# Layer B's second pair of plain projections, five tiles for the reload of the mixer output, and ScalarE's order

## The chip, the cores and the metric

The kernel runs on one NeuronCore of one Trainium2 chip. The metric is the device time of one execution in microseconds (us). TensorE (PE) multiplies matrices, VectorE (DVE), ScalarE (ACT) and GpSimd (POOL) do the elementwise work, SyncE (SP) issues most of the DMAs and ACT's queue some of them. Each engine works through its own list of instructions in order.

## The reference

A decoder trunk of two layers is computed for a prompt of 1024 tokens and 8 sample tokens, 1032 columns in all, at a model width of 1024 and an inner width of 2048, in float32:

```python
hn = rmsnorm(h, norm_mix[i])
# layer A: y = hgrn2_mixer(hn, ...)   chunkwise gated linear recurrence, 8 heads
# layer B: y = chunk_mlp_mixer(hn, ...)
u, v, z = jnp.split(hn @ w_in, 3, axis=-1)
u = gelu(u); v = layernorm(gelu(v), ln_g, ln_b)
s = einsum('gts,bnsgd->bntgd', tril(w_sp), v in chunks of 128) + b_sp
y = (u * s * silu(z)) @ w_out
h = h + y
gate = sigmoid(rmsnorm(h, norm_ple[i]) @ w_ple_gate[i])
h = h + gate * (p[i] @ w_ple_proj[i])
# after both layers: rmsnorm(h, norm_final)
```

Beside the rows of y, the final recurrent states and the last chunk's v rows are returned.

## The kernel before

Activations lie with features on the 128 partitions. The 1032 columns are split into three chunks c = 0, 1, 2 of 384, 384 and 264 columns. Every float32 operand x of a large product is split in two parts, hi (a rounding cast on ScalarE) and lo = x - hi (a subtraction on VectorE or GpSimd), and `mm3` makes three matmuls of it: hi hi, hi lo, lo hi. A weight is treated in the same way by `split_weights`. A projection (`proj`) of one output tile of 128 features and one chunk is thus 8 x 3 = 24 matmuls into one of three PSUM banks that share the tag "mm".

PE's list of instructions is as traced (its schedule is manual). The other engines' lists are put in order by a planner, which simulates the program and takes instructions by priority and expected readiness; `high_priority` moves some forward. Side work that must run between PE's products is written as generators. `Ticks` steps them: `tk.tick()` counts once per half projection or per group, and a generator that yields n goes on n ticks later. The constants SQD, SDEL, NDEL and FDEL are such delays: in `first_norm` SQD is the tick at which a chunk's squares are traced, and SDEL's two numbers are the ticks to the sum over partitions (`norm_sum`, tile pss) and from there to the broadcast (`norm_bc`, tile pbc), after which the normalised rows are split into hi and lo. NDEL does the same for later norms.

The stages that matter here, in order of time:

- The start. p's first projection (`pple`, 12 groups of 6 matmuls, each group emptied from its bank by a ScalarE copy at L301 and stored to DRAM) fills PE while x arrives and is normalised by `first_norm`. Then come the projections fk and qq of head 0, per chunk.
- Layer A, 8 heads. At its end `last_fill` runs p's second projection and the first half of the output projection; `load_zt` brings the mixer output of layer A back from DRAM (tiles ozd), tile by tile, with a cast on ScalarE and a subtraction on VectorE for each.
- Layer B begins while the last norm of layer A is still at work (`norm_rows`, chunk by chunk; chunk 2 last). First one plain pair of v's projections is computed (weights b, MI and MI+1, three chunks each). A Gelu (`vgroup`, L945) makes gv; two ticks later `vstore` transposes it on PE (pt_g, L954), copies it, takes its statistics and stores it. Then `mix` forms sums and differences of the chunks' rows for a Strassen-like scheme and splits them into xm (L900 to L910): four operations and three splits for each of four j, half of them on GpSimd. From then on `unit` computes two output tiles at once, over chunks 0 and 1 by seven products of 12 matmuls in place of eight, and chunk 2 by plain projections. Each unit needs sums of its weights (`load_unit`: four adds on GpSimd, four casts, four subtractions). Units run for the rest of v (m from 2), and then for u and z of each of eight groups g.
- In the last group (g = 7) hooks between the unit's products (`then`) load what the output projection will need: p for layer 1 goes into hh[2], and rows of ozd go into the places of activations that the unit no longer reads. These loads are staged in `wide()` tiles, six buffers named "u", which also hold the gated outputs us until L1147 multiplies them.
- `out_phase` ("ob"): p's last projection (12 groups), with loads of ozd between the groups in stages of three tiles, then the output projection in halves of 8 blocks (tiles ps_o), with the rows of h loaded from DRAM. Then the gate (`ple`) and the final norm.

## Time and profile before

| | us |
|---|---|
| median of 3 runs | 1977.56 (1973.95 to 1980.73) |
| the profiled execution | 1973.68 |
| its span, first to last instruction | 1971.9 |
| PE busy | 1893.8 (96%) |
| VectorE busy | 1182.6 (60%) |
| ScalarE busy | 782.9 (40%) |
| GpSimd busy | 456.8 (23%) |

A row of a timeline gives the start, the length, the engine with line and operation, and, in brackets, how long the engine was idle before it and what released it. Lengths of matmuls are modelled and overlap; how far apart their starts are shows the rate. The granted clock is 1.00 at 2.4 GHz; the lower level is 1.2 GHz. L197 and L196 are the subtraction and the cast inside `split`, L142 and L143 those of `split_weights`, L201 to L203 the three matmuls of `mm3`, and L306 the DMA in `load_split`: many tiles share these lines, so the names of the tiles tell them apart.

### The profile page before, as it was taken

The page shows a single profiled execution, that of the slowest core. Times are in us where ns is not written, and L with a number is a line of the kernel's source. Part 1 is how long each engine was busy: PE and PEld are TensorE (multiplying, and loading weights), DVE is VectorE, ACT ScalarE, POOL GpSimd, SP SyncE. Part 2 cuts the span into 40 slices and gives each one's busy share as a digit, 9 for nine tenths or more (in the row PEclk, how much of TensorE's full clock was granted, in tenths as well). Part 3 has the DMA queues.
Part 4 walks back from the last instruction along what each step waited for, and adds up shares of the span by engine and source line. Part 5 has one row for each costly group of instructions (what it writes and reads, how often), then busy time and mean ns, then how long its engine had stood idle before and what let it go on. Part 6 is the DMA issues. An engine that isn't in the chain of part 4 may idle for free.

```text
span 1971.9 us, 33475 instructions
## 1 busy us (share of the span) xinstructions
PE 1893.8 (96%) x13160; PEld 1852.3 (94%) x13160; DVE 1182.6 (60%) x2610; ACT 782.9 (40%) x1610; POOL 456.8 (23%) x467
## 2 busy tenths in 40 slices
PE   7999999999999998999998899999999996999997
PEld 6999999999999998999998899999999996999997
DVE  5967676776767676311645755587777675311554
ACT  6452535444453536311434544433443344211341
POOL 5110000001000100011323622354444440011221
PEclk8999999999999999999999899999999998999998
DMA  6232322222131326511243333332233238411123
GB/s 207 84 105 71 101 91 79 76 89 97 57 108 59 106 93 217 185 44 44 98 157 111 108 98 92 102 98 95 97 99 105 95 113 262 138 49 44 65 87 107
DMA packets 124076, 203.73 MB, mean 103 GB/s; under 512 B 11600, under 2 KB 96784, under 8 KB 122896
## 3 DMA queue, kind: packets, MB, share of 16 engines
q1 hardware_dynamic: 115280, 191.04, 29.9%
q10 hardware_dynamic: 8640, 10.57, 1.5%
q8 instruction: 103, 1.69, 0.4%
q14 instruction: 53, 0.43, 0.1%
HBM read 148.75 MB, written 52.82 MB: 102 GB/s over the span
## 4 chain that ended last, share of the span: by engine, by line
PE 45%; DVE 7%; DMA 4%; issue 2%; POOL 2%; ACT 2%; SPq 0%; DVEq 0%; POOLq 0%; ACTq 0%
PE ps_proj L202 7%; PE ps_proj L201 7%; PE ps_proj L203 7%; PE ps_o L201 6%; PE ps_o L202 6%; PE ps_o L203 6%; PE ps_d L201 1%; PE ps_d L203 1%; PE ps_d L202 1%; DMA zstg<-ozd 1%; DVE wlo L143 1%; DMA vn<-vraw 1%; DVE bl L197 1%; PE psp L1139 1%; DMA ppd<-pple_t 1%
## 5 line engine op out<-in xcount | busy, mean ns | idle before, releaser
L201 PE MATMUL ps_proj<-bh,whi 128*128 128x384 f32 (+1 forms) x2136 | 689.2, 323 | 8.1 <-ACT pple_t L301 6.7
L202 PE MATMUL ps_proj<-bl,whi 128*128 128x384 f32 (+1 forms) x2136 | 673.3, 315 | 3.8 <-DVE bl L197 2.5
L203 PE MATMUL ps_proj<-bh,wlo 128*128 128x384 f32 (+1 forms) x2136 | 672.9, 315 | 3.1 <-DVE wlo L143 3.1
L201 PEld LDWEIGHTS ps_proj<-bh,whi 128*128 128x128 f32 x2136 | 404.3, 189 | 12.2 <-ACT pple_t L301 6.9
L202 PEld LDWEIGHTS ps_proj<-bl,whi 128*128 128x128 f32 x2136 | 404.8, 190 | 6.6 <-DVE bl L197 3.4
L203 PEld LDWEIGHTS ps_proj<-bh,wlo 128*128 128x128 f32 x2136 | 403.6, 189 | 3.7 <-DVE wlo L143 3.7
L143 DVE TENSOR_TENSOR wlo<-wstg,whi 128x1024 fp32r<-128x1024 f32 x148 | 190.7, 1289 | 152.1 <-ACT whi L142 148.8
L142 ACT CAST whi<-wstg 128x1024 fp32r<-128x1024 f32 x148 | 155.3, 1050 | 130.0 <-PE ps_proj L202 72.3
L234 POOL TENSOR_TENSOR ssq<-ssq,tmp 128x384 f32<-128x384 f32 (+1 forms) x72 | 76.3, 1059 | 419.9 <-ACT tmp L233 372.2
L808 DVE TENSOR_TENSOR h<-h,ps_o 128x384 f32<-128x384 f32 (+1 forms) x48 | 24.5, 511 | 192.9 <-PE ps_o L203 192.9
L142 ACT CAST shi<-ssum 128x512 fp32r<-128x512 f32 x92 | 56.5, 621 | 176.9 <-POOL ssum L172 102.7
L201 PE MATMUL ps_o<-bh,whi 128*128 128x384 f32 (+1 forms) x384 | 123.2, 321 | 2.1 <-ACT pple_t L301 1.6
L202 PE MATMUL ps_o<-bl,whi 128*128 128x384 f32 (+1 forms) x384 | 122.6, 319 | 0.6 <-DVE bl L197 0.6
L233 ACT ACTIVATE tmp<-h 128x384 f32<-128x384 f32 (+1 forms) x72 | 35.3, 490 | 219.5 <-DVE h L808 168.9
L203 PE MATMUL ps_o<-bh,wlo 128*128 128x384 f32 (+1 forms) x384 | 122.4, 319 | 0.0
L143 DVE TENSOR_TENSOR slo<-ssum,shi 128x512 fp32r<-128x512 f32 x92 | 76.7, 833 | 42.9 <-ACT shi L142 42.9
L201 PE MATMUL ps_o<-zh,whi 128*128 128x384 f32 (+1 forms) x288 | 90.0, 313 | 0.0
L202 PE MATMUL ps_o<-zl,whi 128*128 128x384 f32 (+1 forms) x288 | 89.7, 312 | 0.0
L203 PE MATMUL ps_o<-zh,wlo 128*128 128x384 f32 (+1 forms) x288 | 89.7, 311 | 0.0
L589 DVE TENSOR_TENSOR q<-q,t 128x192 f32<-128x192 f32 (+1 forms) x144 | 49.9, 347 | 45.2 <-PE pC L583 43.5
L201 PEld LDWEIGHTS ps_o<-bh,whi 128*128 128x128 f32 x384 | 72.7, 189 | 2.8 <-ACT pple_t L301 2.1
L202 PEld LDWEIGHTS ps_o<-bl,whi 128*128 128x128 f32 x384 | 72.6, 189 | 1.0 <-DVE bl L197 1.0
(278 smaller groups left out, 3904.1 us busy)
## 6 DMA issues: line engine op xcount, KB each, us to landing
wstg<-in_wina SPq DMA_DIRECT2D x48, 512.0 KB, 3.6
wstg<-in_winb SPq DMA_DIRECT2D x48, 512.0 KB, 4.0
zstg<-ozd SPq DMA_DIRECT2D x22, 384.0 KB, 5.7
pj<-ppd SPq DMA_DIRECT2D x16, 516.0 KB, 3.8
S<-in_st SPq DMA_DIRECT2D x16, 512.0 KB, 5.1
vb<-vd SPq DMA_DIRECT2D x16, 512.0 KB, 4.6
out_so_s<-S SPq DMA_DIRECT2D x16, 512.0 KB, 3.4
wstg<-in_wouta SPq DMA_DIRECT2D x16, 512.0 KB, 4.2
```

What stands on the lines that cost most here:

```text
L142: A.copy(hi, src)
L143: V.tensor_tensor(lo, src, hi.bitcast(F32), ALU.subtract)
L197: eng.tensor_tensor(lo, src, hi.bitcast(F32), ALU.subtract)
L201: PE.matmul(ps, wh, xh, start=first, stop=False, skip_group_check=more)
L202: PE.matmul(ps, wh, xl, start=False, stop=False, skip_group_check=more)
L203: PE.matmul(ps, wl, xh, start=False, stop=last, skip_group_check=more)
L233: A.activation(sq[:, :w], src, AF.Square)
L234: eng.tensor_tensor(ssq, ssq, sq[:, :w], ALU.add)
L589: V.tensor_tensor(ql[:, :, 1, :], ql[:, :, 1, :], t2[:, :, 0:1].broadcast_to([P, n, lv]), ALU.mult)
L808: V.tensor_tensor(hr[c][m], hr[c][m], ps[:, :W[c]], ALU.add)
L1139: PE.matmul(pss[:, i, :], vn[:, n0 + i, mm * P:(mm + 1) * P], wst[:, g, :], start=True, stop=True)
```

## The change

- Layer B computes two plain pairs (MI to MI+3) before the first unit, and units of v begin at m = 4. The transposes of these pairs come 4 ticks after the Gelu.
- `mix` becomes a generator that starts once the first pair is done and `norm_rows` has ended. Its operations and the subtractions of its splits all go to VectorE, behind the last norm's last subtraction, one j per tick. The four splits into hh[1] go to VectorE too.
- `load_zt` can issue DMAs `lag` tiles ahead of the cast and can tie each cast behind whatever ScalarE was given last (`keep_in_program_order`: an order of issue, without a wait). The tie is the default and thus holds at the end of layer A also.
- In the last group the rows of ozd are staged in five tiles "zq" of their own, five ahead, without the tie. cv is formed in place in gb.
- `out_phase` allocates its staging pool first, loads one tile after each group with a lag of two, and takes chunk 2's rows 0 to 7 into new tiles and 8 to 15 into hh[2].
- At the start the staging of p has three tiles, pple_t six, the squares of chunks 1 and 2 are tied behind a PSUM copy and behind a split, and SQD, SDEL and NDEL have other delays.

```diff
 NWARM = 12
+ZQ = 5
 FDEL = ((2, 2), (2, 4), (1, 3))
-SQD = (0, 5, 9)
+SQD = (0, 6, 12)
 OD = (4, 4)
-SDEL = ((6, 3), (6, 2), (6, 2))
-NDEL = (((1, 3), (1, 4), (2, 3)), ((2, 4), (2, 6), (2, 6)))
+SDEL = ((6, 4), (7, 2), (5, 2))
+NDEL = (((1, 3), (1, 4), (2, 3)), ((2, 4), (2, 6), (3, 6)))
 OFF = (0, 384, 768)
 W = (384, 384, 264)
 NT = (3, 3, 2)
...
     order += [("g", 0, m) for m in range(KT)]
     order += [("p", 1, 0)]
-    order += [("b", MI), ("b", MI + 1)] + [("B", MI + m) for m in range(2, MI, 2)]
+    order += [("b", MI + m) for m in range(4)] + [("B", MI + m) for m in range(4, MI, 2)]
...
@@ -192,9 +193,11 @@
         return loaded[n]
 
 
+    last = {}
+
     def split(hi, lo, src, eng=V):
-        A.copy(hi, src)
-        eng.tensor_tensor(lo, src, hi.bitcast(F32), ALU.subtract)
+        last["split"] = A.copy(hi, src)
+        last["lo"] = eng.tensor_tensor(lo, src, hi.bitcast(F32), ALU.subtract)
...
 
-    def load_p(ap, l, c, ph, pl):
-        stg = ap.tile([P, 2, 384], F32, name="pstg", bufs=2)
+    def load_p(ap, l, c, ph, pl, bufs=2):
+        stg = ap.tile([P, 2, 384], F32, name="pstg", bufs=bufs)
         nc.sync.dma_start(stg[:, :, :W[c]], pT[l][:, :, OFF[c]:OFF[c] + W[c]])
         ph[c] = ap.tile([P, 2, W[c]], F32R, name=f"ph{c}")
...
                     mm3(ps[:, :W[c]], blk(wh, b), blk(wl, b), ph[c][:, k, :], pl[c][:, k, :], k == 0, k == 1)
                 t = tp.tile([P, 384], F32, name="pple_t", tag=stg[0], bufs=stg[1])
-                A.copy(t[:, :W[c]], ps[:, :W[c]])
+                last["pple"] = A.copy(t[:, :W[c]], ps[:, :W[c]])
                 nc.scalar.dma_start(ppd[l][4 * half + mm][:, OFF[c]:OFF[c] + W[c]], t[:, :W[c]])
...
@@ -306,13 +309,24 @@
         nc.sync.dma_start(stg, src)
         split(hi, lo, stg)
 
-    def load_zt(zt, parts, stage, n=2):
-
-        for c, k0 in parts:
-            zh, zl, nk = zt[c, k0]
-            for k in range(0, nk, n):
-                load_split(zh[:, k:k + n, :], zl[:, k:k + n, :], ozd[c][:, k0 + k:k0 + k + n, :], stage(W[c]))
-                yield
+    def load_zt(zt, parts, stage, n=2, lag=0, tie=True):
+
+
+        todo = [(c, k0, k) for c, k0 in parts for k in range(0, zt[c, k0][2], n)]
+        stg = []
+        for i in range(len(todo) + lag):
+            if i < len(todo):
+                c, k0, k = todo[i]
+                stg.append(stage(W[c]))
+                nc.sync.dma_start(stg[i], ozd[c][:, k0 + k:k0 + k + n, :])
+            if i >= lag:
+                c, k0, k = todo[i - lag]
+                zh, zl, _ = zt[c, k0]
+                hi = A.copy(zh[:, k:k + n, :], stg[i - lag])
+                if tie:
+                    tc.keep_in_program_order(hi)
+                V.tensor_tensor(zl[:, k:k + n, :], stg[i - lag], zh[:, k:k + n, :].bitcast(F32), ALU.subtract)
+            yield
 
...
@@ -366,24 +380,27 @@
 
     load(0)
     ph, pl = [None] * 3, [None] * 3
-    load_p(sp, 0, 0, ph, pl)
-    load_p(sp, 0, 1, ph, pl)
+    load_p(sp, 0, 0, ph, pl, 3)
...
-    fill = pple(0, sp, ph, pl, 0, ("pple_t", 4))
+    fill = pple(0, sp, ph, pl, 0, ("pple_t", 6))
 
     def first_norm(c):
-        yield SQD[c]
+        if c:
+            yield SQD[c]
         sq = sp.tile([P, KT, 384], F32, name="sq0", bufs=2)[:, :, :W[c]]
         for j in range(0, KT, 2):
-            A.activation(sq[:, j:j + 2, :], xs[c][:, j:j + 2, :], AF.Square)
+
+            with tc.issue_after(last["pple" if c == 1 else "split"].ins) if c else ExitStack():
+                A.activation(sq[:, j:j + 2, :], xs[c][:, j:j + 2, :], AF.Square)
             (V if c == 0 else G).tensor_tensor(sq[:, j, :], sq[:, j, :], sq[:, j + 1, :], ALU.add)
             if j:
                 (V if c == 0 else G).tensor_tensor(sq[:, 0, :], sq[:, 0, :], sq[:, j, :], ALU.add)
...
         with ExitStack() as s:
+            st = stage2(pool(s, "zstg"), 3)
             zp = pool(s, "oz")
 
             def load_h(m):
@@ -782,17 +800,13 @@
                     for c in CH:
                         nc.sync.dma_start(hr[c][m], src[:, OFF[c]:OFF[c] + W[c]])
 
-            st = stage2(pool(s, "zstg"), 3)
             for c, k0, nk in parts:
                 zt[c, k0] = (zp.tile([P, nk, W[c]], F32R, name=f"zh{c}_{k0}"),
                              zp.tile([P, nk, W[c]], F32R, name=f"zl{c}_{k0}"), nk)
-            todo = load_zt(zt, late, st)
-            if fill is not None:
-                for i, _ in enumerate(fill):
-                    if i % 2:
-                        tk.tick()
-                        next(todo, None)
-                run(load_zt(zt, [(2, 0)], st))
+            todo = load_zt(zt, late, st, 2, 2 if fill else 0)
+            for _ in fill or ():
+                next(todo, None)
+                tk.tick()
             run(todo)
             for m in range(4):
                 load_h(m)
...
                 split(out[0][c][:, j, :], out[1][c][:, j, :], t, V if j % 2 else G)
+        last["norm"] = last["lo"]
 
...
 
         for j in range(4):
-            e = V if j % 2 else G
             b11, b12, b21, b22 = hr[0][j], hr[1][j], hr[0][j + 4], hr[1][j + 4]
-            e.tensor_tensor(b11, b12, b11, ALU.subtract)
-            e.tensor_tensor(b12, b22, b12, ALU.subtract)
-            e.tensor_tensor(b22, b22, b11, ALU.subtract)
-            e.tensor_tensor(b21, b21, b22, ALU.subtract)
-            for i, t in ((1, b22), (0, b11), (2, b12)):
-                split(xm[i][0][:, j, :], xm[i][1][:, j, :], t, G if (i + j) % 2 else V)
+            with tc.issue_after(last["norm"].ins):
+                V.tensor_tensor(b11, b12, b11, ALU.subtract)
+                V.tensor_tensor(b12, b22, b12, ALU.subtract)
+                V.tensor_tensor(b22, b22, b11, ALU.subtract)
+                V.tensor_tensor(b21, b21, b22, ALU.subtract)
+                for i, t in ((1, b22), (0, b11), (2, b12)):
+                    split(xm[i][0][:, j, :], xm[i][1][:, j, :], t)
+            yield 1
 
     with ExitStack() as sG:
         ep = pool(sG, "pj")
...
         return wb.tile([P, 384], F32, name="u", bufs=6)
 
-    def vgroup(m, c, src):
+    def vgroup(m, c, src, d=2):
         w = W[c]
         gv = wide()
         A.activation(gv[:, :w], src, AF.Gelu_apprx_tanh)
         if c == 2:
             G.tensor_copy(gvs[:, m, :], gv[:, 256:264])
-        tk.spawn(vstore(m, c, gv), 2)
+        tk.spawn(vstore(m, c, gv), d)
 
     def vstore(m, c, gv):
 
...
         yield
 
 
-    wv = take("b", MI), take("b", MI + 1)
-    for c in CH:
-        for m in range(2):
-            ps = proj(wv[m], hh[c], hl[c], c)
-            vgroup(m, c, ps[:, :W[c]])
-            tk.tick()
-    while any(p[2].__name__ == "norm_rows" for p in tk.procs):
+    for q in range(0, 4, 2):
+        wv = take("b", MI + q), take("b", MI + q + 1)
+        for c in CH:
+            for m in range(2):
+                ps = proj(wv[m], hh[c], hl[c], c)
+                vgroup(q + m, c, ps[:, :W[c]], 4)
+                tk.tick()
+        if q == 0:
+            while any(p[2].__name__ == "norm_rows" for p in tk.procs):
+                tk.tick()
+            tk.spawn(mix(), 1)
+    while any(p[2].__name__ == "mix" for p in tk.procs):
         tk.tick()
-    mix()
     for j in range(4):
-        split(hh[1][:, j, :], hl[1][:, j, :], hr[0][j + 4], G if j % 2 else V)
+        split(hh[1][:, j, :], hl[1][:, j, :], hr[0][j + 4])
     load(taken[0])
     sH.close()
 
...
 
-    for m in range(2, MI, 2):
-        unit(take("B", MI + m), lambda i, c, src: vgroup(m + i, c, src), early=m == 2)
+    for m in range(4, MI, 2):
+        unit(take("B", MI + m), lambda i, c, src: vgroup(m + i, c, src), early=m == 4)
...
         nc.sync.dma_start(gb[:, 1, :], lnbr[g].partition_broadcast(P))
-        cv = wb2.tile([P, DV], F32, name="cv", bufs=1)
-        G.tensor_tensor(cv, vn[:, 7, :], gb[:, 0, :], ALU.mult)
+        cv = gb[:, 0, :]
+        G.tensor_tensor(cv, vn[:, 7, :], cv, ALU.mult)
         G.tensor_tensor(cv, cv, gb[:, 1, :], ALU.add)
         nc.sync.dma_start(cv_p[:, g * DV:(g + 1) * DV], cv)
...
             zt = {(0, 0): (hh[0], hl[0], 8), (1, 0): (*xm[1], 4), (1, 4): (*xm[0], 4), (1, 8): (*xm[2], 4),
-                  (0, 8): (hh[1], hl[1], 8), (2, 0): (hh[2], hl[2], 8)}
+                  (0, 8): (hh[1], hl[1], 8), (2, 8): (hh[2], hl[2], 8)}
             ph, pl = p_in_act(1, None, False)
 
-            def fetch(c, k0):
-                return lambda: run(load_zt(zt, [(c, k0)], lambda w: wide()[:, :w].rearrange("p (k t) -> p k t", k=1), 1))
-
-            spatial(g, vn, us, take("B", 2 * MI + 2 * g),
-                    (lambda: p_in_act(1, lambda w: ws[0].tile([P, 512], F32, name="ssum", bufs=2)[:, :w]), None, fetch(1, 0), fetch(0, 0), fetch(1, 4),
-                     fetch(1, 8)))
+            zq = load_zt(zt, [(1, 0), (0, 0), (1, 4), (1, 8)],
+                         lambda w: wb2.tile([P, 384], F32, name="zq", bufs=ZQ)[:, :w].rearrange("p (k t) -> p k t", k=1),
+                         1, ZQ, False)
+
+            def fetch(n):
+                return lambda: [next(zq, None) for _ in range(n)]
+
+            def first():
+                fetch(ZQ)()
+                p_in_act(1, lambda w: ws[0].tile([P, 512], F32, name="ssum", bufs=2)[:, :w])
+
+            spatial(g, vn, us, take("B", 2 * MI + 2 * g), (first, None, fetch(4), fetch(8), fetch(4), fetch(ZQ + 4)))
     sB.close()
 
     sH, hr, sp = open_rows()
     ssq3 = new_ssq()
     act3 = new_act()
     out_phase("ob", zt, ssq3, False, lambda c: norm_spawn(c, ssq3, 3, act3, NDEL[0]), {},
-              [(1, 12, 4), (2, 8, 8)], [(0, 8), (1, 12), (2, 8)], pple(1, sp, ph, pl, 1, ("tmp", 4)))
+              [(1, 12, 4), (2, 0, 8)], [(2, 0), (0, 8), (1, 12), (2, 8)], pple(1, sp, ph, pl, 1, ("tmp", 4)))
 
     with ExitStack() as sE:
```

## Rows read from the trace of the kernel before

**Rows 1.** Page, parts 1 and 2: PE's busy us, share; tenths by slice.
```profile
PE 1893.8 (96%) x13160; PEld 1852.3 (94%) x13160; DVE 1182.6 (60%) x2610; ACT 782.9 (40%) x1610; POOL 456.8 (23%) x467
...
PE   7999999999999998999998899999999996999997
```

**Rows 2.** Waits of PE, whole span: us in total, times, longest.
```profile
PE ps_pple L201 <- ACT pple_t L301: 21.4, 8, 12.8
...
PE ps_proj L201 <- ACT pple_t L301: 6.7, 1, 6.7
...
PE pt_g L954 <- ACT u L945: 6.6, 2, 4.0
```

**Rows 3.** Windows: length, busy us by engine (instructions), clock, DMA share, GB/s.
```profile
8.00:40.00 32.00, 20.68 (x118) 19.62 (x119) 19.43 (x36) 20.90 (x39) 20.44 (x21) 0.84 0.75 259
...
740.00:780.00 40.00, 33.80 (x231) 31.10 (x230) 28.45 (x57) 28.96 (x70) 4.20 (x5) 1.00 0.62 195
...
1060.00:1120.00 60.00, 45.92 (x251) 44.05 (x251) 46.54 (x76) 33.79 (x74) 41.20 (x37) 0.86 0.31 94
...
1620.00:1640.00 20.00, 20.00 (x138) 20.00 (x138) 13.52 (x27) 9.69 (x20) 3.84 (x4) 1.00 0.56 170
...
1640.00:1690.00 50.00, 33.21 (x181) 31.27 (x180) 25.21 (x40) 25.40 (x45) 3.58 (x3) 0.83 0.89 289
```

**Rows 4.** Timeline of PE, start: start us, us, instruction, [idle before <- releaser].
```profile
34.09 0.52 PE L202 MATMUL ps_proj<-bl,whi 128*128 128x384 f32 x1
...
34.41 0.52 PE L203 MATMUL ps_proj<-bh,wlo 128*128 128x384 f32 x1
...
37.48 0.83 PE L257 MATMUL pbc<-ident,rsq 128*128 128x128 f32 x6
...
38.33 0.34 PE L202 MATMUL ps_proj<-bl,whi 128*128 128x384 f32 x1
...
38.50 0.34 PE L203 MATMUL ps_proj<-bh,wlo 128*128 128x384 f32 x1
```

**Rows 5.** Timeline of ACT, start.
```profile
33.19 0.65 ACT L301 COPY pple_t<-ps_pple 128x264 f32<-128x264 f32 x2
```

**Rows 6.** Timeline of POOL, start.
```profile
34.77 1.00 POOL L197 TENSOR_TENSOR bl<-tmp,bh 128x384 fp32r<-128x384 f32 x1
...
44.42 2.58 POOL L197 TENSOR_TENSOR bl<-tmp,bh 128x384 fp32r<-128x384 f32 x2
```

**Rows 7.** Timeline of PE, layer B's first projections.
```profile
1070.17 0.70 PE L246 MATMUL pss<-ones,ssq 128*128 128x1 f32 x6 [3.36 <-DVE ssq L231]
...
1093.74 0.90 PE L954 MATMUL pt_g<-ident,u 128*128 128x128 f32 x3 [4.01 <-ACT u L945]
...
1111.76 0.55 PE L954 MATMUL pt_g<-ident,u 128*128 128x128 f32 x3 [2.58 <-ACT u L945]
```

**Rows 8.** Timeline of ACT, layer B's first projections.
```profile
1091.37 0.51 ACT L196 CAST xmh<-h 128x384 fp32r<-128x384 f32 x1 [3.19 <-POOL h L907]
```

**Rows 9.** Groups of DVE by form, 1076 to 1112: busy us, mean ns.
```profile
L197 DVE TENSOR_TENSOR xml<-h,xmh 128x384 fp32r<-128x384 f32 x6 | 6.3, 1086 | 0.0
...
L908 DVE TENSOR_TENSOR h<-h,h 128x384 f32<-128x384 f32 x2 | 1.1, 534 | 0.0
```

**Rows 10.** Groups of DVE by form, 1130 to 1250.
```profile
L959 DVE BATCH_NORM_STATS2 stats<-u 128x6 f32<-128x128 f32 x81 | 18.5, 281 | 7.3 <-ACT u L956 7.3
...
L143 DVE TENSOR_TENSOR wlo<-wstg,whi 128x1024 fp32r<-128x1024 f32 x11 | 13.5, 1230 | 13.0 <-ACT whi L142 13.0
```

**Rows 11.** Waits of SP's queue, 1615 to 1660.
```profile
SPq L306 <- POOL s L1147: 12.0, 6, 5.3
```

**Rows 12.** Timeline of ACT, reload.
```profile
1657.90 0.83 ACT L196 CAST bh<-zstg 128x768 fp32r<-128x768 f32 x1 [4.19 <-DMA zstg<-ozd]
...
1685.12 0.63 ACT L196 CAST bh<-zstg 128x528 fp32r<-128x528 f32 x1 [1.52 <-DMA zstg<-ozd]
```

**Rows 13.** Timeline of PE, the output projection's first matmul.
```profile
1672.58 0.69 PE L201 MATMUL ps_o<-bh,whi 128*128 128x384 f32 x1
```

3 lines of the change are left out of this document (2 added, 1 removed).

## The prediction

> **What bounds the kernel now.** I read the page first: TensorE (PE) is busy 96% of the span and its slices are nines almost throughout [rows 1]. Time can therefore come from two sources only: fewer matmuls, or the stretches where PE idles and then restarts at the lower clock level. So next I read PE's waits over the whole span [rows 2] and, in windows, the stretches where they lie [rows 3]. The reader should see four of them. 8 to 40 us (the start) has 32 - 20.68 = 11.3 us without a matmul; 740 to 780 (end of layer A) 6.2; 1060 to 1120 (layer B's first projections, where the activations' sums are made) 14.1; 1640 to 1690 (the reload of the mixer output) 16.8. Last I read who PE waited for in each, engine by engine.
>
> Idle time costs a second time: after long waits the granted clock stays at 1.2 GHz for a while. Beside the 6.7 us wait at the start, 384-column matmuls begin 0.32 us apart at first and 0.17 apart later [rows 4]; 9 to 15 of them, or as many narrower ones, go by in each such stretch, so one costs 1.3 to 2.0 us. The trace has one at the start, four in 1060 to 1120 and two in 1640 to 1690, which fits the mean clocks 0.84, 0.86 and 0.83 [rows 3].
>
> **The change part by part.** The sum is made against the profiled execution: 1973.68 us, a span of 1971.9 and 1.8 around it. The median of the three runs, 1977.56, lies 3.9 above it; I add that at the end.
>
> *Reload (1640 to 1690), the largest term.* In the last pair of layer B the earlier rows of the mixer output come back from DRAM through the six "u" tiles, which still hold the gated outputs. SP's queue stood 12.0 us in six waits until POOL's multiply had released one [rows 11]. ScalarE then had the casts of these late loads, and a cast of the next stage (1657.90, after 4.19 us idle for its DMA), in its queue ahead of the copies that empty the PSUM banks [rows 12]; PE needs those copies and stood 12.8 us [rows 2]. In the change the loads get five tiles of their own with the issue five ahead of the cast; the staging pool is allocated first; chunk 2's first half moves to fresh tiles, so it no longer waits for the tile that holds p; and each later cast is tied behind the PSUM copy traced before it, two loads behind its own DMA. What could be gained at most: 16.8 us idle and two clock stretches of 1.4, together 19.6. What the transfers allow: 289 GB/s at a share of 0.89 means the same bytes would need 50 x 0.89 = 44.5 us at full share, 5.5 us less; in 1620 to 1640 the share is 0.56, so 20 x 0.44 = 8.8 us of transfer time lies free, which the early issue can use [rows 3]. Sum 14.3; I take -14. Bounds: -5.5 (nothing starts earlier, only the gaps close) and -19.6; the tie's own danger is a rival below.
>
> *Layer B's first projections (1060 to 1120).* Four waits, in order. First, PE waits 3.36 us for chunk 2's sum of squares [rows 7]. NDEL moves that step one tick, i.e. two groups of p's projection later: 12 matmuls of 0.17 = 2.1 us go in front of the wait, 1.3 remains, and the clock stretch behind it (1.6) should not come: -3.7. Second, a wait of 2.75 for the second weight's low part and its clock stretch: not touched, 0. Third, 4.01 us for a Gelu output [rows 7]: ScalarE stood 3.19 us in a cast of the activations' sums, which waited for GpSimd, with the Gelu queued behind it [rows 8]. The sums are now traced after the first pair, beside the second: -4.0 and -2.0 for the clock. Fourth, 2.58 us of the same kind [rows 7]: -2.6 and -1.5. Together -13.8.
>
> What this costs: a plain pair has 2 x 2 x 24 = 96 matmuls of 384 columns and 48 of 264; the unit that it replaces has 7 x 12 = 84 and 48. Twelve more, 12 x 0.17 = +2.1 us, all on PE. And the sums need cover. VectorE gets 4 x (4 + 3) + 4 = 32 operations of 384 columns. One takes 0.53 us alone (the L908 row) and 1.09 on average where GpSimd works beside it [rows 9]: 17 to 35 us. Beside them VectorE does 16 statistics of 0.28, four weight low parts of 1.23 [rows 10] and four half-width ones, taken as 0.7 each: 12.2 us. The cover is pair 2 (96 x 0.17 + 48 x 0.12 = 22.1 us), the next unit's two chunk-2 projections (5.8) and its first product (2.0), 29.9 us until PE needs the sums. Uncontended that is 29 against 30, at the contended price 47 against 30: 0 to +17. GpSimd has no part in the sums any more and only the next unit's four weight sums, so I take nearly the low end, +1. The term: -13.8 + 2.1 + 1 = -10.7, say -11; bounds -12 and about +5. The longer delay (4 ticks instead of 2) before the transposes holds one or two more of six "u" tiles; I cost it at nothing, since no unit runs then; if the tiles ran out, each Gelu would wait for a transpose, about one projection half, 2 us.
>
> A rule of the Trainium skill speaks against my cheap price. "SBUF — State Buffer", section "Who interferes with whom", says that a VectorE instruction with two SBUF inputs and a GpSimd instruction that reads SBUF block each other for the whole instruction. By it, VectorE would still stand for the unit's weight sums on GpSimd, and the term would be some 4 us worse (a total near 1952). The spread of 0.53 to 1.09 us agrees with it [rows 9]; no row shows the sums on VectorE alone.
>
> *Start (8 to 40).* PE waited 6.7 us for a PSUM bank whose copy stood at 33.19 on ScalarE behind all eight casts of chunk 0 [rows 2, 5]. With SDEL's 4 in place of 3 the normalisation of chunk 0 is traced one group later, so that bank's copy comes before the casts. What is late next is chunk 0's last low part: GpSimd made it at 34.77, after chunk 2's sums of squares [rows 6]; those are now tied behind the casts, which should bring it to about 31. PE then begins paced by the low parts and ends its first projection near 34 in place of 40. But chunk 1's broadcast, at 37.48 in the middle of that projection [rows 4], moves one projection down, to about 36; from it to the last low part of chunk 1 passed 44.42 + 2.58 - 37.48 = 9.5 us [rows 4, 6], so the third projection can end near 46, not 50. I take -4. Bounds: +1 (one more clock stretch; chunk 1 and 2's squares stand behind a copy that waits) and -10 (nearly all of the 11.3 idle). The third staging tile for p and two more tiles for its copies remove small waits that lie inside this; a transfer-bound start (share 0.75) cannot give more.
>
> *End of layer A (740 to 780).* The loads there now carry the tie too, which keeps casts behind the PSUM copies; the 6.2 us idle [rows 3] are shared by several causes, copies one of them, so I take a sixth: -1, bounds +2 and -3. The copy of cv in place costs nothing: its store has some 40 us until the tile is loaded again.
>
> Sum: -14 - 11 - 4 - 1 = -30. 1973.7 - 30 = 1943.7, and with 3.9 for the median 1947.6: I forecast **1947.5 us**.
>
> **The rivals.**
> *A, the transfers still set the reload.* For it: 0.89 of all DMA time is taken there and SP issues in order, so weights and rows of h stand behind loads that wait for tiles. Against: the 12.0 us of waits on POOL vanish. Reload -5.5 in place of -14: 1956.
> *B, the sums outlast their cover.* For it: 29 against 30 us has no slack. Against: GpSimd leaves. Ten microseconds late at the first product of sums, with a clock stretch: -11 becomes about +1, 1959.
> *C, the tie turns each copy into a wait for a transfer; slower.* Place: p's last projection in the reload. Ten casts are now queued between twelve PSUM copies; ScalarE waits for each cast's DMA with the copies behind it. In the trace ten such casts landed between 1657.90 and 1685.12 [rows 12], 27.2 us, 2.7 each. If each took a whole wait of 4.2, as the one at 1657.90, ten would take 42 us from 1653.7 to 1695.7, and PE would begin the output projection 23 us later than now (it began at 1672.58 [rows 13]). With the other terms' -16: +7, 1984.5. It decides from about 3.5 us a cast (35 - 19 = 16). Against: two loads of lag and a staging pool that no longer lies where late tiles stood.
> *D, it doesn't do what it says.* The ties fix only who is behind whom; the planner orders the rest anew, and waits of the old size come back elsewhere: within 0.3%, 1976.
>
> **How the numbers follow.** Forecast 0.60 (own range 1936 to 1955), A 0.18, B 0.10, C 0.06, D 0.06. Faster: 0.60 + 0.18 + 0.10 = 0.88; same 0.06; slower 0.06. About 0.3%, 6 us, is what a measurement of this kernel can tell from no change. Range: the terms' better ends (-19.6, -12, -10, -3, together 1933) are its lower bound. Upwards it takes in A and B, nearly both at once (1947.5 + 8.5 + 11.5 = 1967.5): 1966. Outside lie C, D and little else.
>
> **What would show it.** Reload right: no PE wait over 3 us between p's last projection and the first output matmul, SP's waits on L1147 gone. Projections right: no wait of pt_g for a Gelu over 1 us, 12 more matmuls in all, the sums on VectorE at 0.53 to 0.6 us each and ending before the first product of sums. Start right: the first projection's matmuls begin before 31 us, and paced by low parts. Wrong: a PE wait over 8 us at the first product of sums (B), PSUM copies spaced by DMA waits (C), or PE idle time in the four stretches still above 40 us in total (D).

## The result and the profile after

The changed kernel takes 1964.5 us (median of 4 runs, 1960.9 to 1966.3) against 1978.4 for the kernel before beside it (1974.0 to 1980.7): a ratio of 0.993, interval 0.9907 to 0.9953. Run again (5 runs, below) it took 1967.4, a ratio of 0.9947 (0.9935 to 0.9960). The gain is thus 10 to 14 us. I forecast 1947.5, a gain of 30; the stated range, up to 1966, held this time, and the second value lies 1.4 above it. The profiled executions stand at 1966.3 and 1973.7 (spans 1964.5 and 1971.9).

First the same windows of the kernel after as in [rows 3] (length, busy us by engine, granted clock, DMA share, GB/s).

```profile
8.00:40.00 32.00, 24.92 (x137) 22.76 (x138) 18.33 (x35) 23.48 (x43) 19.41 (x19) 0.95 0.76 262
740.00:780.00 40.00, 33.04 (x215) 30.13 (x213) 25.16 (x53) 26.07 (x65) 4.09 (x5) 0.96 0.64 209
1060.00:1120.00 60.00, 55.95 (x367) 54.33 (x366) 49.29 (x98) 35.56 (x74) 20.57 (x19) 1.00 0.33 106
1620.00:1640.00 20.00, 20.00 (x131) 20.00 (x131) 17.04 (x34) 12.08 (x26) 5.99 (x4) 1.00 0.74 228
1640.00:1690.00 50.00, 38.31 (x214) 36.83 (x214) 22.65 (x32) 20.47 (x37) 1.00 (x1) 0.90 0.82 269
```

The third did what was forecast: 60 - 55.95 = 4.1 us idle in place of 14.1, clock 1.00 in place of 0.86. The last kept 11.7 idle of 16.8. The first looks good and misleads, as will be seen. PE's waits over the whole span (us, times, longest), beside [rows 2]:

```profile
PE ps_pple L204 <- ACT pple_t L304: 18.3, 7, 4.0
...
PE po L204 <- ACT junk L635: 3.0, 1, 3.0
...
PE pt_g L970 <- ACT u L972: 1.8, 2, 1.3
```

The waits for copies of p's projections were 21.4 and are 18.3, over the three places where p is projected. Between 1640 and 1690 us alone they were 15.7 in four and are 10.5 in three: the longest is broken up, not gone.

Windows shift when the kernel does, so from here on I measure from one event to the next. *Start*: until head 0's state is stored. *End of A*: from head 6's state to the first matmul of the ones (pss) behind layer A's output projection. *B's front*: from there to the first spatial matmul (psp) of group 0. Then psp of group 0 to group 1, of 1 to 6, and *reload*: from group 6's psp to the first pss behind layer B's output projection. What lies between them stays within 0.4 us, what lies behind within about 1.1. All runs, each stretch from one profile, in us; the ratios are medians against the kernel before in the same rounds:

| run | start | end of A | B's front | 0 to 1 | 1 to 6 | reload | ratio (95%) |
|---|---|---|---|---|---|---|---|
| before | 140.9 | 269.8 | 354.7 | 46.4 | 228.1 | 267.7 | 1 |
| after | 141.4 | 276.2 | 341.9 | 50.0 | 227.0 | 262.8 | 0.9930 (0.9907 to 0.9953) |
| e1 | 141.3 | 272.0 | 341.9 | 48.9 | 227.2 | 261.7 | 0.9927 (0.9913 to 0.9942) |
| e2 | 141.6 | 272.8 | 341.9 | 49.2 | 227.6 | 261.1 | 0.9925 (0.9907 to 0.9944) |
| e3 | 142.0 | 271.9 | 343.8 | 47.1 | 226.8 | 260.4 | 0.9919 (0.9904 to 0.9934) |
| e4 | 142.4 | 275.4 | 343.4 | 49.2 | 226.8 | 254.3 | 0.9898 (0.9882 to 0.9914) |
| e5 | 143.0 | 272.9 | 344.1 | 48.8 | 226.8 | 263.0 | 0.9947 (0.9935 to 0.9960) |
| e6 | 141.8 | 270.4 | 341.9 | 47.0 | 226.4 | 266.3 | 0.9922 (0.9908 to 0.9937) |
| e7 | 142.3 | 272.9 | 347.0 | 48.9 | 226.6 | 261.2 | 0.9951 (0.9938 to 0.9964) |
| e8 | 141.5 | 269.8 | 341.8 | 48.5 | 227.4 | 258.3 | 0.9881 (0.9866 to 0.9896) |
| e9 | 141.0 | 268.9 | 343.4 | 49.4 | 227.3 | 254.1 | 0.9878 (0.9865 to 0.9891) |
| e10 | 142.0 | 275.3 | 343.4 | 48.5 | 226.2 | 257.1 | 0.9908 (0.9894 to 0.9921) |
| e11 | 142.1 | 271.6 | 343.5 | 49.6 | 227.9 | 262.1 | 0.9942 (0.9929 to 0.9954) |
| e12 | 142.1 | 270.6 | 341.8 | 49.0 | 227.4 | 254.0 | 0.9883 (0.9869 to 0.9897) |

In the reload of the kernel after, PE, ScalarE and SyncE's queue show who holds whom (timelines: start, length, instruction, idle before and releaser):

```profile
1648.45 0.69 PE L204 MATMUL ps_pple<-bh,whi 128*128 128x384 f32 x1 [3.98 <-ACT pple_t L304]
...
1656.12 0.44 PE L204 MATMUL ps_pple<-bh,whi 128*128 128x384 f32 x1 [2.94 <-ACT pple_t L304]
...
1663.17 0.59 PE L204 MATMUL ps_pple<-bh,whi 128*128 128x264 f32 x1 [3.60 <-ACT pple_t L304]
```

```profile
1647.51 0.52 ACT L1172 ACTIVATE sg<-u 128x384 f32<-128x384 f32 x1 [2.26 <-DVE u L1086]
1647.94 0.46 ACT L304 COPY pple_t<-ps_pple 128x384 f32<-128x384 f32 x1
...
1650.07 0.48 ACT L304 COPY pple_t<-ps_pple 128x384 f32<-128x384 f32 x1 [0.43 <-ACT pple_t L304]
1654.63 0.33 ACTq L305 DMA_DIRECT2D ppd<-pple_t  x1
1655.05 0.63 ACT L325 CAST zh<-zstg 128x528 fp32r<-128x528 f32 x1 [4.50 <-DMA ozd<-s]
1655.59 0.47 ACT L304 COPY pple_t<-ps_pple 128x384 f32<-128x384 f32 x1
...
1659.84 0.33 ACTq L305 DMA_DIRECT2D ppd<-pple_t  x1
1662.11 0.63 ACT L325 CAST zh<-zstg 128x528 fp32r<-128x528 f32 x1 [3.60 <-DMA zstg<-ozd]
1662.65 0.85 ACT L304 COPY pple_t<-ps_pple 128x384 f32<-128x384 f32 x2
```

```profile
1636.72 0.94 SPq L321 DMA_DIRECT2D zstg<-ozd  x2
...
1649.77 0.32 SPq L1175 DMA_DIRECT2D ozd<-s  x1
1650.18 6.17 SPq L801 DMA_DIRECT2D h<-hd  x8
1656.45 0.38 SPq L321 DMA_DIRECT2D zstg<-ozd  x1
```

The first wait ends with a copy behind a sigmoid that waited for VectorE.

The second looks like a cast that waits for its reload, and is not: that reload was one of the two issued at 1636.72, and both had landed by 1642.24. What the copy stands behind is the issue of the previous copy's store (L305 at 1654.63), which is in ScalarE's own list. In the trace each of the 625 DMAs reports its end on one of eight semaphores (counters that instructions wait for), in turn over both queues, and an issue waits until the DMA before it on its semaphore has ended. For this L305 that was a store of s, issued by SyncE at 1649.77 and landed at 1654.55, with which it shares no data. All six profiles with the changed order in this stretch (after, e1, e2, e5, e7, e11) show such a hold, of 3.9 to 4.3 us; e3, e4, e8, e9, e10 and e12 do not.

In the third wait, 1.3 of the 3.60 us are again such an issue (1659.84) and 2.0 are the reload of the cast. That reload was issued at 1656.45, behind eight rows of h, and its staging tile came free only at 1656.4, by the low part that belongs to the cast held before.

The Trainium skill's "PSUM — Partial Sum Buffer", section "Engine vs sequencer instructions", says that ScalarE's queue is strictly first in, first out. The rows agree: a copy of 0.47 us stood 4.5 us behind an issue and a cast that it does not need.

At the end of layer A the same tie shows (ScalarE, PE, SyncE of the kernel after):

```profile
766.20 0.48 ACT L304 COPY pple_t<-ps_pple 128x384 f32<-128x384 f32 x1 [3.12 <-DMA ppd<-pple_t]
...
767.24 0.83 ACT L325 CAST bh<-zstg 128x768 fp32r<-128x768 f32 x1 [0.56 <-ACT pple_t L304]
...
768.28 0.83 ACT L325 CAST bh<-zstg 128x768 fp32r<-128x768 f32 x1
...
769.28 0.38 ACT L635 ACTIVATE junk<-po 128x256 f32<-128x256 f32 x1
```

```profile
769.81 0.39 PE L204 MATMUL po<-vh,ah 128*128 128x256 f32 x1 [3.01 <-ACT junk L635]
```

```profile
758.97 5.58 SPq L321 DMA_DIRECT2D zstg<-ozd  x5
```

Here casts tied between copies delay the recurrence of head 7 (junk frees po's only bank), and a copy waits 3.12 us for the store of an older one, beside five reloads of which three are the output phase's; before the change these three were issued only after 782 us (SyncE of the kernel before):

```profile
782.24 1.50 SPq L306 DMA_DIRECT2D zstg<-ozd  x3
```

### The profile page after: what moved, and what is told of

Its sections match the earlier page's. It is cut to its first block, busy times and chain, and to the rows that moved or that the text cites. A ratio compares the mean times of both kernels' runs of the same rounds, so it can differ in the third digit from the quotient of the medians.

```text
span 1964.5 us, 33449 instructions
## 1 busy us (share of the span) xinstructions
PE 1898.8 (97%) x13172; PEld 1853.6 (94%) x13172; DVE 1173.0 (60%) x2617; ACT 780.0 (40%) x1605; POOL 434.5 (22%) x447
## 4 chain that ended last, share of the span: by engine, by line
PE 74%; DVE 10%; DMA 7%; issue 3%; ACT 3%; POOL 2%; SPq 0%; DVEq 0%; ACTq 0%; POOLq 0%
PE ps_proj L205 14%; PE ps_proj L204 14%; PE ps_proj L206 14%; PE ps_o L204 6%; PE ps_o L205 6%; PE ps_o L206 6%; DMA wstg<-in_winb 2%; DVE wlo L144 2%; DMA ppd<-pple_t 1%; PE pC L600 1%; PE ps_d L204 1%; PE ps_d L206 1%; PE ps_d L205 1%; DVE sg L1173 1%; PE p L580 1%
## 5 line engine op out<-in xcount | busy, mean ns | idle before, releaser
L205 PEld LDWEIGHTS ps_proj<-bl,whi 128*128 128x128 f32 x2160 | 407.0, 188 | 13.4 <-POOL bl L200 8.9
L205 PE MATMUL ps_o<-zl,whi 128*128 128x384 f32 (+1 forms) x288 | 89.7, 312 | 0.0
L206 PE MATMUL ps_o<-zh,wlo 128*128 128x384 f32 (+1 forms) x288 | 89.7, 311 | 0.0
```

Of the source, the lines that this page charges most:

```text
L205: PE.matmul(ps, wh, xl, start=False, stop=False, skip_group_check=more)
L206: PE.matmul(ps, wl, xh, start=False, stop=last, skip_group_check=more)
```

## Experiments

**e1: no tie in layer A.**
```
-  run(load_zt(zt, [(c, 0)], stage2(wa, 2)))
+  run(load_zt(zt, [(c, 0)], stage2(wa, 2), tie=False))     # last_fill and out_phase "oa" likewise
```


> Edit of the changed kernel: the casts of the reloads in layer A are no longer tied behind the ScalarE instruction traced before them; layer B's keep the tie. In the changed kernel the end of layer A (from head 6's state to the first matmul of the ones behind layer A's output projection) takes 6.4 us longer than before. Theory 1 (the tie does it: casts that wait for a transfer stand ahead of the PSUM copies on ScalarE): this stretch gets back 5 to 6.5 us, the first matmul of the ones comes at 949 to 951 us instead of 955.8, the median falls by about 6 us. Rival (the loads themselves or the small pool for p's copies, two tiles each, hold the copies, and the tie is only beside it): the stretch stays within 1.5 us of the changed kernel, the waits of PE for copies at 780 to 786 us stay.


Measured: head 7's state comes 88.7 us after head 6's, as before (88.8; with the tie 89.7 to 91.4). The stretch takes 272.0. But e2 to e4, which share the changed code there, took 272.8, 271.9 and 275.4: the 276.2 of the first profile was not typical, and the median hardly moved. By this one profile the tie costs something, and about 2 us remain without it.

**e2: own-tile reloads late.**
```
-                fetch(ZQ)()
+                with tc.issue_after(gd.ins):      # gd: the load of group 7's bias
+                    fetch(ZQ)()
```


> Edit of the changed kernel: the first five reloads into the five own tiles are tied on SyncE's queue behind the load of group 7's gain and bias, so that none of them can be issued in group 0, where the trace of the changed kernel has two (1321.13 us). From group 0's first spatial matmul to group 1's the changed kernel lost 3.6 us against before. Theory 1 (these two loads collide with the group's weight and vn loads and delay the weight sums): 3 to 4 us come back, group 1's first spatial matmul stands 50 us after group 0's -3.6 = about 46.4 us as before, the median falls by 3 to 4 us. Rival (the group's own weight loads or cv in place do it): the distance stays at 50 us, the median within 1 us.


Measured: 49.2, within the 47.1 to 50.0 of the kernels that keep the early reloads. The theory fell: no effect of them is shown.

**e3: rows of h behind the last reload.**
```
-  nc.sync.dma_start(hr[c][m], src[...])
+  with tc.issue_after(last["zd"].ins) if fill else ExitStack():
+      nc.sync.dma_start(hr[c][m], src[...])
```


> Edit of the changed kernel: in layer B's output phase the loads of the residual rows h are tied on SyncE's queue behind the last reload of the mixer output. In the changed kernel the copies that empty PSUM in p's last projection wait behind casts for reloads (4.50 us idle at 1655.05 and 3.60 at 1662.11), and the reloads of those casts were issued between rows of h. Theory A (transfers set the reload: the reloads came late because rows of h were ahead of them): PE's waits of 2.9 and 3.6 us shrink together by 3 us or more, the stretch by 3 to 5 us. Theory C (the order on ScalarE alone sets it: a tied cast takes a whole transfer each, whoever is ahead): less than 1.5 us.


Measured: reload 260.4, against the six profiles with the changed order there (after, e1, e2, e5, e7, e11: 261.1 to 263.0, mean 262.0) 1.6 us less. That is near theory C's figure. But PE's waits of 2.94 and 3.60 became these:

```profile
1652.61 0.39 PE L204 MATMUL ps_pple<-bh,whi 128*128 128x264 f32 x1 [0.17 <-ACT pple_t L304]
1656.99 0.59 PE L204 MATMUL ps_pple<-bh,whi 128*128 128x264 f32 x1 [2.67 <-ACT pple_t L304]
```

Together that is 3.7 us less, as theory A had it, and the output projection's first matmul comes 88.6 us after group 6's psp instead of 92.6 us. Some of it is lost again, as the granted clock behind the 2.67 us is 0.57 from 1658 to 1664 us, in the output projection. The wait that is left is the tie's: the copy stands behind a cast that waits 2.04 us for its reload. So neither theory is enough alone. Issuing the rows of h last also shifts which DMAs share a semaphore, and the hold of 4 us went with it; the two are not separated.

**e4: copies first.** As e3, and in addition:
```
             for _ in fill or ():
-                next(todo, None)
                 tk.tick()
             run(todo)
```


> The kernel with the rows of h last (the run beside this one), and in addition every late reload's cast is traced behind the last of the twelve PSUM copies of p's last projection, so that no copy stands behind a cast that waits for a transfer. Theory C (casts between the copies turn copies into waits for transfers): PE's waits for copies of 2.9 and 3.6 us and the slow clock behind them go, the output projection's first matmul comes at about 1658 instead of 1667.5, and since its first two thirds need no late reload (8 us of matmuls), the first matmul of the ones behind it comes 5 to 8 us earlier than in the changed kernel (1837.5). Theory A (the transfers set the end, whatever the order): the output projection starts earlier but waits as long for chunk 2's rows; the gain is below 2 us.


Measured: reload 254.3, 7.7 less than the mean of 262.0 and 8.5 less than in the first profile, as theory C had it for the two edits together; beside e3 the copies' place gives 6.1. All of PE's waits from 1640 to 1690 us, and SyncE's late reloads:

```profile
1643.63 0.44 PE L204 MATMUL ps_pple<-bh,whi 128*128 128x384 f32 x1 [0.95 <-DVE u L1082]
1648.93 0.69 PE L204 MATMUL ps_pple<-bh,whi 128*128 128x384 f32 x1 [3.99 <-ACT pple_t L304]
```

```profile
1662.59 1.56 SPq L321 DMA_DIRECT2D zstg<-ozd  x3
...
1666.91 6.55 SPq L321 DMA_DIRECT2D zstg<-ozd  x4
```

The waits of 2.94 and 3.60 are gone. The reloads are issued *later* than in the kernel after, and PE still does not wait for one: the output projection has enough work that needs none. The transfers do not bound the reload, though e3 shows that the order in which they are issued counts while casts stand between the copies.

**e5: the changed kernel again** (no edit).


> The changed kernel itself once more, for how much its stretches vary from execution to execution. In the four profiles that share its code there, the end of layer A (head 6's state to the first matmul of the ones behind the output projection) took 6.4, 3.1, 2.1 and 5.6 us more than before. Theory (the stretch has several marginal waits and a restart at the lower clock that comes in some executions only): again between 2 and 6.5 us, and the distance from group 0's to group 1's first spatial matmul between 47 and 50 us (46.4 before); the median is 1961 to 1965 us. Rival (the first profile was typical, 6.4 and 50.0 are the kernel's values): within 0.5 us of both.


Measured: end of A 272.9, group 0 to 1 48.8, median 1967.4. The first profile was the worst of its kind at the end of A; that stretch varies by 4 us from execution to execution.

**e6: layer B's front alone**, in the kernel before (NDEL, the order of weights, `mix` on VectorE as a generator, two plain pairs; nothing else).


> The kernel before with layer B's first projections alone changed: two plain pairs, the sums of the activations beside the second on VectorE, the later transposes. Nothing of the start, of layer A's end, of the own tiles and of cv in place. Theory: the stretch from the last matmul of the ones in layer A's gate phase to group 0's first spatial matmul gets shorter by 11 to 13 us as in the changed kernel (354.7 before, 341.9 after), and the stretch from group 0 to group 1 stays at 46 to 47 us as before, so the median falls by 11 to 13 us. Rival (the group 0 to 1 stretch loses its 2 to 3.6 us because the groups are reached in another state, not because of reloads or cv): that stretch takes 48 to 50 us here too, and the median falls by only 8 to 10.


(The 354.7 is counted from the first ones-matmul behind layer A's output projection, as in the table, not from the gate phase.) Measured: 341.9, -12.9 us, as in the whole change. Group 0 to 1 takes 47.0. The median, 1961.99 against 1977.39, is -15.4: this part alone is 5.4 us faster than the whole change in the same rounds (1967.40). So all the other parts together gave nothing in these rounds, or cost some us; against the first pair (0.9930) the difference is 1.6 us, and the intervals overlap.

**e7: sums on both engines.**
```
+            e = V if j % 2 else G           # the four sums on e, each split on G if (i + j) % 2 else V
```


> Edit of the changed kernel: the sums of the activations and their low parts alternate between VectorE and GpSimd, as they did before, at the new place beside the second plain pair. Theory 1 (the place does it: the sums have 30 us of cover, whoever makes them): the stretch to group 0's first spatial matmul stays within 1.5 us of the changed kernel's 341.9 us. Theory 2 (VectorE alone does it: with both engines each operation takes 1.1 us instead of 0.54 and the casts on ScalarE wait for GpSimd again, with Gelu outputs behind them): the stretch loses 4 us or more, and waits of the transposes for a Gelu of over 1.5 us come back.


Measured: 347.0, 5.2 more than in the first profile of the kernel after and 2.9 more than in its second (e5). The medians of the same rounds, 1967.9 and 1967.4, show no difference. One operation of the sums by form (busy us, mean ns), first the kernel after, then e7:

```profile
L923 DVE TENSOR_TENSOR h<-h,h 128x384 f32<-128x384 f32 x4 | 3.2, 812 | 0.0
L922 DVE TENSOR_TENSOR h<-h,h 128x384 f32<-128x384 f32 x4 | 2.2, 546 | 0.0
L921 DVE TENSOR_TENSOR h<-h,h 128x384 f32<-128x384 f32 x4 | 2.2, 544 | 0.0
L920 DVE TENSOR_TENSOR h<-h,h 128x384 f32<-128x384 f32 x4 | 2.1, 540 | 0.0
```

```profile
L200 POOL TENSOR_TENSOR xml<-h,xmh 128x384 fp32r<-128x384 f32 x6 | 6.7, 1118 | 5.8 <-ACT xmh L199 3.1 <-DMA vraw<-u 2.7
L199 ACT CAST xmh<-h 128x384 fp32r<-128x384 f32 x12 | 5.8, 510 | 10.2 <-POOL h L923 5.2 <-DVE h L922 2.9 <-DVE h L921 2.1
...
L922 DVE TENSOR_TENSOR h<-h,h 128x384 f32<-128x384 f32 x2 | 2.4, 1214 | 0.0
L921 DVE TENSOR_TENSOR h<-h,h 128x384 f32<-128x384 f32 x2 | 1.9, 961 | 0.0
```

The 5.2 us of the profiles would be theory 2's size; the medians do not bear it out. What the profiles do show is the price of an operation: VectorE alone takes 0.54 us an operation and 0.89 to 1.21 beside GpSimd's (one form stays at 0.54), and ScalarE's casts wait 10.2 us, 5.2 of them for GpSimd's sums. But theory 2's waits for a Gelu do not come back: pt_g waits 0.26 for one, and 0.33 for the copy that empties its bank. PE's longer waits are for weights' parts, 0.77 and 1.36, with the lower clock, and one of 3.70 in place of 2.12 lies ahead of the sums, which the new order of work explains and not the sums.

**e8: local edits at four places.** e4's edits; e1's edit with the staging pool of layer A behind the tiles; e2's edit with `ZQ = 4` and cv in a tile of its own; `SDEL[1] = (6, 1)`.
```
-            st = stage2(pool(s, "zstg"), 3)
+            if not first: st = stage2(pool(s, "zstg"), 3)
             zp = pool(s, "oz")
+            if first: st = stage2(pool(s, "zstg"), 3)
```


> The changed kernel with edits at four places far apart, each read by its own stretch. Reload: copies first and rows of h last, as measured (-8.5 us in the stretch). End of layer A: no tie on the casts and the output phase's staging pool allocated behind its tiles again, so that none of its loads can start beside p's copies. Theory: that stretch returns to 269.8 us, as before (272.0 with the tie gone alone). Rival (something else in the changed kernel holds p's copies): it stays at 272 or more. Group 0: the own-tile reloads behind group 7's gain and bias, four own tiles instead of five, and cv in a tile of its own. Theory: from group 0 to group 1 returns to 46.4 us; rival (neither is the cause): 47 to 50. Start: chunk 1's statistics and broadcast one step earlier on TensorE (after 12 matmuls of the first projection, as before, instead of 36). Theory (the broadcast's place gave the gain back): the first head's state is stored 2 to 4 us earlier than 141.4; rival (low parts on GpSimd pace it whatever the order): within 1 us. In all about -14 us against the changed kernel if every theory holds: 1947 to 1951 us.


Measured: end of A 269.8, as before to 0.1 us: theory. Group 0 to 1 48.5: rival, but 1.6 of it is the clock behind a wait that is as long as in e6 (last section). Start 141.5, within the spread of the others: rival. Reload 258.3, 4 more than e4. Median 1953.7, a little above what was expected. In the reload PE and ScalarE show where it is lost:

```profile
1644.91 0.69 PE L204 MATMUL ps_pple<-bh,whi 128*128 128x384 f32 x1 [8.98 <-ACT pple_t L304]
```

```profile
1642.96 1.52 ACT L325 CAST xmh<-zq 128x384 fp32r<-128x384 f32 x3 [4.25 <-DMA zq<-ozd]
```

The copy stands behind casts out of the tiles zq, which wait for their reloads.

**e9: mended version.** e4's reload with five tiles, cv in place, e8's end of A, and the decay bounds' chain (`lb`) moved behind chunk 0's normalisation.
```
-    V.tensor_tensor(lb[:, 1, :], ...)            # the chain, ahead of fk
+    for _ in fill: tk.tick()
+    with tc.issue_after(last["lo"].ins):         # the same chain
```


> The changed kernel with copies first and rows of h last in the reload, layer A's end without the tie and with the staging pool behind its tiles (five own tiles and cv in place kept), and at the start the small chain that makes layer A's decay bounds moved on VectorE behind chunk 0's normalisation; in the changed kernel it stands ahead of it from 25.2 to 26.7 us. Theory (VectorE's normalisation paces the first projection): the first head's state is stored 1 to 2 us earlier than in the six profiles with this start (141.25 to 143.04, mean 142.0). Rival (what paces it is GpSimd or the clock): within 0.7 us of 142.0. Reload stretch (group 6's first spatial matmul to the first matmul of the ones behind layer B's output projection): 254.3 us as with copies first and five own tiles; the previous run had 258.3 with four own tiles and late reloads, and if the number of own tiles is not the reason it stays at 258. End of layer A 269.8. Median 1947 to 1951 us.


Measured: start 141.0, 1 us below the mean of 142.0 and 0.3 below the best: undecided. Reload 254.1, so e8's loss comes with its four tiles, the late issue into them and cv's own tile, which were not separated (e2's late issue alone lost nothing). Median 1952.6, -24.0 us.

**e10: shared tiles.** As e4, with the reloads through `wide()` and each cast at once.
```
-  lambda w: wb2.tile([P, 384], F32, name="zq", bufs=ZQ)[...], 1, ZQ, False)
+  lambda w: wide()[...], 1, 0, False)
```


> The kernel with copies first and rows of h last (reload stretch 254.3 us), but the reloads of the earlier rows go through the six shared tiles of the gated outputs as they did before, each cast at once, without the issue five ahead. Theory 1 (own tiles are needed: SyncE's queue stands again on GpSimd's gating multiply, and the late reloads behind it come late): the stretch gets 4 us or more longer, SyncE's waits on the gating multiply return at some 10 us. Theory 2 (the order on ScalarE and of the rows of h was everything): within 1.5 us of 254.3.


Measured: 257.1, 2.8 more than e4, between the two. SyncE's waits on GpSimd's multiply are back (11.3 us in six, as in [rows 11]), and PE's one wait for a copy is 8.55 in place of 3.99. So the order, together with the changed staging and chunk 2's fresh tiles, is the larger part: from 267.7 to 257.1 without own tiles, to 254.3 with them.

**e11: pool behind, tie kept.** e8's edit of the pool alone.


> The changed kernel with layer A's staging pool allocated behind the output phase's tiles, as before, and the tie kept. End of layer A: 269.8 us before; 271.9 to 276.2 in the seven profiles of the changed code there (mean 273.7 without the untied one), 272.0 with the tie gone and the pool in front, 269.8 with the tie gone and the pool behind. If the two causes add, this takes 271 to 272.5; if the pool's place alone is the cause, 269.8; if the tie alone, 273 or more. The rest of the kernel as in the changed one, the median 1961 to 1966 us.


Measured: 271.6. With tie and pool in front 271.9 to 276.2 (seven profiles, mean 273.9); no tie 272.0; neither 269.8, 268.9, 270.6. By these the two add, about 2 us each; but e1 and e11 are one profile each of a stretch that varies by 4 us.

**e12: as e9 with the start as before the change.**


> As the run with the late decay bounds, but with the start exactly as before the change (four staging tiles for p's copies, two for p, the squares untied, the delays of before). Theory (the new start gives nothing, on average it costs about 1 us): first head's state at 140.9 to 141.8 us, and the median within 1.5 us of the run with the late decay bounds. Rival (the new start does gain once the decay bounds are out of the way): that run is faster by 2 us or more. Everything else as there: reload 254.3, end of layer A 269.8, median 1946 to 1951 us.


Measured: 142.1 and a median of 1952.9, the same as e9. The start of before stands at 140.9, 141.8 and 142.1, the new one at 141.0 to 143.0 in eleven profiles (two of them with edits).

## Why the prediction was partly wrong

**Layer B's first projections: right, for the reasons given.** Forecast -11, measured -12.9 and, where one clock stretch came in addition, -10.6 to -11.3. PE of the kernel after:

```profile
1077.35 0.70 PE L249 MATMUL pss<-ones,ssq 128*128 128x1 f32 x6 [0.58 <-DVE ssq L234]
...
1088.50 0.45 PE L206 MATMUL ps_proj<-bh,wlo 128*128 128x384 f32 x1 [2.12 <-DVE wlo L144]
...
1125.79 0.55 PE L970 MATMUL pt_g<-ident,u 128*128 128x128 f32 x3 [1.32 <-ACT u L972]
```

The wait for chunk 2's sum fell from 3.36 to 0.58, and the second low part still waits 2.12. Of pt_g's waits for a Gelu, 4.01 and 2.58 [rows 7], none is left: its 1.32 and 0.46 are for the copy that empties its bank (L972). PE has 13172 matmuls, twelve more, as said. VectorE took 0.54 us an operation, the cheap price of [rows 9]. The rule of the Trainium skill's "SBUF — State Buffer", section "Who interferes with whom", which spoke against it, agrees with the rows where both engines run (L923's mean 0.81; e7's 0.89 to 1.21). Its price of 4 us did not come, as GpSimd's weight sums met only the last few operations.

**Reload: -14 forecast, -4.9 in the first pair, -5.7 on average. This is the step that failed most**, in the clause "each later cast is tied behind the PSUM copy traced before it, two loads behind its own DMA", taken as removing the wait. The tie fixes a cast's place between two copies and says nothing of what the cast, or anything else in ScalarE's list, waits for. What the runs show in its place: PE's waits for copies fell by a third only, from 15.7 to 10.5 us, and the sign that I named, no PE wait over 3 us, failed with 3.98 and 3.60. Behind the second wait is the issue of a store on ScalarE's own queue, held 4.0 us by a DMA of SyncE's queue, which I had not thought of; behind the third are such an issue (1.3 us) and a tied cast whose reload came late (2.0 us). The tied cast is rival C's mechanism, at 2.0 us here and in e3's last wait, where C had 23 in all; C got 6 in 100, since I priced all ten casts at one wait each. That the potential was sized right e4 shows: with the rows of h last and all copies ahead of the casts the stretch is -13.4 (254.3 against 267.7). Rival A is refuted by the same run as a bound of the transfers; that the order of their issue does not matter is not shown, as e3 got 3.7 us of waits back by it. About 4 us of wait remain at the first copy; in the kernel after it is the one behind the sigmoid (1647.51), and VectorE was making low parts of reloads among others then. This I did not test.

**End of layer A: -1 forecast, +2 to +6 measured** (mean +4.1 over the seven profiles). I counted "copies one of them" of the 6.2 us idle and did not ask what else the new lines reach there. Two things: the tie, which `load_zt` has by default and which here holds the recurrence as well as the copies; and "the staging pool is allocated first", which I costed only in layer B. In layer A it gives the tiles an earlier free place, so three transfers start 20 us earlier, beside the stores of p's copies. The second and third of these stores take 4.0 to 5.3 us to land in the eight profiles with the pool in front, 1.9 to 2.4 in five of the other six and 3.6 in e6. e8, e9 and e12 show that both together make the loss (268.9 to 270.6 without them); the share of each rests on single profiles.

**Start: -4 forecast, nothing measured.** The first projection does begin earlier and is paced by low parts, as said (PE of the kernel after):

```profile
27.92 0.44 PE L204 MATMUL ps_proj<-bh,whi 128*128 128x384 f32 x1 [0.16 <-ACT bh L199]
...
38.32 0.83 PE L260 MATMUL pbc<-ident,rsq 128*128 128x128 f32 x6
...
50.30 0.92 PE L260 MATMUL pbc<-ident,rsq 128*128 128x128 f32 x6
```

But I put chunk 1's broadcast at 36 and the third projection's end near 46. The broadcast came at 38.3 (37.5 before [rows 4]) and chunk 2's at 50.3 (47.1). From 40 to 60 us PE is busy 18.5 in place of 20.0 (windows, before and after):

```profile
40.00:60.00 20.00, 20.00 (x134) 19.82 (x133) 17.75 (x42) 14.22 (x31) 10.25 (x14) 1.00 0.18 59
```

```profile
40.00:60.00 20.00, 18.49 (x116) 16.57 (x115) 15.76 (x39) 12.39 (x27) 10.84 (x17) 1.00 0.14 45
```

It arrives early and waits there. An earlier 27.92 was worth nothing as long as chunks 1 and 2 were not normalised earlier. Neither the broadcast's place (e8) nor the decay bounds (e9) moved it by more than 1 us; what would is open.

**Not foreseen: groups 0 to 1, +0.6 to +3.6.** I had costed cv in place and the own tiles at nothing there. One wait for VectorE, 1.70 before, is 2.0 to 2.7 (3.1 in e11) in every kernel with the new front; with the early reloads and cv in place gone (e8) it is 2.03, as in e6. The larger part, 1.6 us, is the clock behind that wait, in 11 of 13 profiles (next section). Why the wait grew by 0.3 in e6 is not settled.

With the means over the profiles that keep each part as changed, -5.7 (reload), -12.0 (front), +4.1 (end of A), +2.6 (groups 0 to 1), -1.1 (groups 1 to 6) and +0.4 (start, 142.0 against 141.6) make -11.7, within the measured -10 to -14.

## What to carry to other kernels

On an in-order engine, an instruction that waits for a transfer belongs behind the ones that free another engine's buffers, not between them: here that was worth some 6 us, and nearly 8 with the rows of h issued last, where the new buffers gave 2.8. The issue of a DMA is such an instruction too, when the engine's own queue issues it: ask which earlier DMA, on whichever queue, it waits for. When a shared helper or a pool's place is changed, look at each caller: a place that frees earlier also starts transfers earlier. And an engine that starts earlier gains only if what it needs next comes earlier too.

## What was not expected of the hardware

The same wait is followed by the lower clock in one execution and not in another. In e6 and e8 PE waits 2.03 us at the same place of group 0; here are the two waits and the 6 us behind each, first e6, then e8:

```profile
1329.71 0.44 PE L203 MATMUL ps_d<-bh,whi 128*128 128x384 f32 x1 [2.03 <-DVE c L1064]
```

```profile
1328.94 0.45 PE L204 MATMUL ps_d<-bh,whi 128*128 128x384 f32 x1 [2.03 <-DVE c L1079]
```

```profile
1329.51:1335.71 6.20, 6.00 (x42) 6.01 (x43) 3.16 (x5) 2.97 (x5) 1.64 (x2) 1.00 0.29 87
```

```profile
1328.74:1334.94 6.20, 6.00 (x31) 6.00 (x32) 3.21 (x5) 2.20 (x4) 1.64 (x2) 0.72 0.22 85
```

42 matmuls at clock 1.00 against 31 at 0.72: 1.6 us, about all of the difference of that stretch (47.0 and 48.5). e3 waited 2.40 without it; the kernel before, 1.70, without it. B's front has its two values, 341.9 and 343.4, in the same way: behind a wait of 2.11 us e8 starts 23 matmuls within 4 us at clock 1.00, e9 14 at 0.57. A wait of this size costs 1.6 us more or not, by chance as far as these runs tell; two profiles that differ by less than that at one wait show nothing about an edit.
